# Splitting weight blocks ahead: a later split, a second raw place, one block per step

## The chip, the core and the metric

The kernel runs on one core of a Trainium2 chip. Its time is the device time of one execution in microseconds (us). The core has a matrix engine (PE, with its weight loads shown as PEld), three engines for elementwise work (DVE, ACT and POOL), and SP, whose queue issues nearly all DMAs of this kernel, one after the other. Each engine takes its instructions strictly in the order that the program gives it; semaphores make one wait for another.

## The reference, cut to what matters

Two groups of 2048 tokens pass through one encoder layer with shared weights:

```python
h = rms_norm(x, norm_w)
q_a, k_a, v_a, g_a, q_b, k_b, v_b, g_b = split(h @ w_in)     # 1024 x 3328
o_a = windowed_gqa_sink(rope(norm(q_a)), rope(norm(k_a)), v_a) * silu(g_a)
o_b = neighbourhood_attn(norm(q_b), norm(k_b), v_b, rpb_b) * silu(g_b)
x = x + concat([o_a, o_b]) @ w_out
y = x + (p @ w_ple) * sigmoid(x @ w_ple_gate)
```

Everything is float32. A product is formed from two parts of each operand: the rounded value (high) and what the rounding left (low), as three matmuls: high x high, high x low and low x high. So every operand, weights too, has to be split into two parts before PE can use it. A split of a 128x512 block is one ACT instruction (the high part) and one DVE instruction (raw minus high).

## The kernel before, in words

The work is a series of steps f, one for each block of 128 tokens. Steps 0 to 31 are stage A (projection and windowed attention of both groups). Steps 32 to 95 are stage B: 32 steps with the first half of the heads of group B, then 32 with the second half. A last stage, C, does the output projection and the gate.

The order of PE's instructions is fixed by a plan. A generator (`filler`) gives the projection matmuls of a step one by one, 24 to a projection. In stage B there are two projections per step: pqk (queries and keys, weights wa) and pvg (values and gates, weights wb). Between these matmuls the plan places the attention of a step six earlier: scores (scb), transposes of the probabilities (ptb), and the products with the values (pob). The attention hangs on DVE and ACT: DVE adds the bias to a score and takes the maximum (s, mx, line 263), ACT takes the exponential (s, line 279), ACT and DVE split the transposed probabilities (p_t, lines 838 and 839), and PE's pob needs p_t.

The rest of the engines' orders comes from a scheduler that keeps the program's priorities; a DMA is placed as early as its buffers allow.

The weight blocks that later stages need are split ahead, once, and their two parts are stored to DRAM (tensors named sp_...). This is `presplit` (lines 207 to 223). There are 44 such blocks: 28 of w_in for stage B, 4 of w_ple and 12 of w_out. `presplit(True)`, called at matmul 4 of a projection (PA), takes a tile "pre" of 128x3x512 with one buffer and loads a raw block of 256 KB into its third place. `presplit(False)`, 16 matmuls later in the same projection, has ACT and DVE write the two parts into the first two places, pinned behind the matmul that stands there (`behind`), and issues the store of 512 KB. As the tile has one buffer, the next load waits until that store has landed. In stage A one block is split per step, in steps 2 to 29.

From step 32 on a second user takes the same buffer (tag "raw"): `combine` (line 581) builds sums of the blocks of w_out and w_gate, eight of them, each in six moves: two loads of 512 KB, four POOL subtractions or additions, a store of 1 MB. One move is made per step, so it ends in step 80. Only then (`combined`) are the last 16 blocks split, in both projections of each step, two blocks per step, in steps 81 to 88.

Two steps at a change of weights run as a pair (`paired`): 62 and 63, between which the weights of the second half are loaded, and 94 and 95. In the latter pair the two 128x512 blocks of the first operand of p @ w_ple (p_r) are split as jobs between matmuls; `hold` counts how many matmuls pass before the first.

Other names: stx is a block of x on its way in; vb are values that are stored to DRAM (v_d) and loaded again as vw; o_tb is an output, stored to ob_d; kb and qg are normed keys and queries; q1b and q are the two parts of the queries.

Of the kernel before, what the change touches and what calls it, by code (L numbers as in the profile page):

```python
# [11 lines left out]
F32 = mybir.dt.float32  # L12
F32R = mybir.dt.float32r
# [6 lines left out]
NT = SEQ // 128  # L20
# [56 lines left out]
PA = 4  # L77
# [4 lines left out]
HOLD = {"wa": 20, "wb": 12, "wp": 0}  # L82
# [18 lines left out]
def emit(ctx, tc, io):  # L101
    nc = tc.nc
# [13 lines left out]
    nw = cp.tile([128, KT], F32, tag="nw", name="nw")  # L116
# [46 lines left out]
    jobs, hold, step = [], [0], [2]  # L163
# [16 lines left out]
    def w_block(half, tag, j):  # L180

        if half == "p":
            return io["w_ple"][128 * j:128 * j + 128, 512 * tag:512 * tag + 512]
        if half == "o":
            h, c = int(tag[2]) - 1, int(tag[1]) - 1
            return io["w_out"][512 * h + 128 * j:512 * h + 128 * j + 128, 512 * c:512 * c + 512]
        c0 = 1280 + 1024 * half + (512 if tag == "wb" else 0)
        return io["w_in"][128 * j:128 * j + 128, c0:c0 + 512]
# [13 lines left out]
            ws.append(w)  # L202
        return ws

    pre = []

    def presplit(load):

        if load:
            if to_split:  # L210
                pre.append((to_split.pop(0), ap.tile([128, 3, 512], F32R, tag="raw", name="pre", bufs=1)))
                nc.sync.dma_start(pre[-1][1][:, 2].bitcast(F32), w_block(*pre[-1][0]))
        elif pre:
            key, t = pre.pop()
            raw, sc = t[:, 2].bitcast(F32), nw[:, key[2]:key[2] + 1]
            if key[0] in ("p", "o"):
                behind(nc.scalar.copy(t[:, 0], raw))
                behind(nc.vector.tensor_tensor(out=t[:, 1], in0=raw, in1=t[:, 0].bitcast(F32), op=ALU.subtract))
            else:
                behind(nc.scalar.activation(t[:, 0], raw, AF.Copy, scale=sc))  # L220
                behind(nc.vector.scalar_tensor_tensor(out=t[:, 1], in0=raw, scalar=sc, in1=t[:, 0].bitcast(F32),
                                                      op0=ALU.mult, op1=ALU.subtract))
            nc.sync.dma_start(parts_d[key], t[:, 0:2].bitcast(F32))

    def load_first(st, j, c, n):

# [83 lines left out]
    ap = ab_stack.enter_context(tc.tile_pool(name="ab", bufs=1))  # L310
# [76 lines left out]
    raw = ap.tile([128, 4, 512], F32, tag="raw", name="ws", bufs=1)  # L387
# [23 lines left out]
    for i in range(2):  # L411
        square(1, i)
    blocks = [(half, tag, j) for half in range(2) for tag in ("wa", "wb") for j in range(KT)]
    parts_d = {(half, tag, j): dram.tile([128, 2, 512], F32, tag=f"sp_{half}{tag}{j}", name=f"sp_{half}{tag}{j}")
               for half, tag, j in blocks if half == 0 or tag == "wa" or j % 2 == 0}
# [3 lines left out]
    to_split = list(parts_d)  # L419
# [25 lines left out]
    for i in range(2):  # L445
        t = ap.tile([128, 2, 512], F32R, tag=f"q2{i}", name=f"q2{i}")
# [24 lines left out]
    def proj_a(f):  # L471
        s, t = divmod(f, NT)
# [80 lines left out]
        for i, c in enumerate(project(pg, xr, lambda k, b: w_g[k][:, b, :], 215)):  # L553
            if i in HG and f > 0 and not early:
                split(f + 1, HG[i], low=nc.vector if f == 1 else nc.gpsimd)
            if i in HN and f > 0 and f not in last:
                square(f + 1, HN[i])
            if i == PR:
                queries()
            if i in (PA, PA + 16) and 1 < f < 2 * NT - 2:  # L560
                presplit(i == PA)
            yield c
            if i + 24 == ka:
                keys_a(kt, t)
# [35 lines left out]
    combining, combined = combine(), []  # L600
# [106 lines left out]
    def proj_b(f):  # L707
        half, st = divmod(f - 2 * NT, 2 * NT)
        s, j = divmod(st, NT)
        b, cb = divmod(j, 4)  # L710
        if f < 2 * NT + 8:
            regroup_next()
        if not ks_b:
            ks_b.extend(big([128, 32, 2, 64], F32R, f"ks_b{e}") for e in range(2))
        w_qk, w_vg = w_b[half]
        xr = xt.pop(f)
        pk = ptile([128, 512], "pj", "pqk")
        for i, c in enumerate(project(pk, xr, lambda k, b: ready("wa", k, w_qk)[:, b, :], 215)):
            at = i + 24 if f in last else i
            if i == PD and f == 2 * NT + 9:  # L720
                stats_b(1)
            if at in HX:
                split(f + 1, HX[at])
            if i in (PA, PA + 16) and combined and f < 6 * NT - 2:
                presplit(i == PA)
            yield c
        sq = ap.tile([128, 512], F32, tag="sq", name="sqb", bufs=2)
        nc.scalar.activation(sq, pk, AF.Square)
        ssq = ap.tile([128, 8], F32, tag="ssq", name="ssqb", bufs=3)
        nc.vector.tensor_reduce(out=ssq, in_=sq.rearrange("p (h d) -> p h d", d=HD), op=ALU.add, axis=AX.X)  # L730
        vr = ap.tile([128, 8], F32, tag="vr", name="vrb", bufs=2)
        y = ap.tile([128, 8], F32, tag="y", name="yb", bufs=4)
        nc.vector.tensor_scalar(out=vr, in0=ssq, scalar1=1.0 / HD, scalar2=ep_b[:, st:st + 1],  # L733
                                op0=ALU.mult, op1=ALU.add)
        rsqrt(vr, y, 8)
        qg = ap.tile([128, 2, 4, HD], F32, tag="qg", name="qg", bufs=6)
        kt = ap.tile([128, 4, HD], F32, tag="kt", name="kb", bufs=2)
        def normed():

            for dst, c in ((kt, 4), (qg[:, 0], 0)):  # L740
                behind(nc.vector.tensor_tensor(out=dst, in0=pk[:, 64 * c:64 * c + 256].rearrange("p (h d) -> p h d", d=HD),
                                               in1=y[:, c:c + 4].unsqueeze(2).broadcast_to([128, 4, HD]), op=ALU.mult))
        yield 0, False
        pv = ptile([128, 512], "pj", "pvg")
        for i, c in enumerate(project(pv, xr, lambda k, b: ready("wb", k, w_vg)[:, b, :], 215)):
            if i + 24 in HX and f not in last:
                split(f + 1, HX[i + 24])
            if i == (PR if f not in last else 1):
                normed()
            if i in (PA, PA + 16) and combined and f < 6 * NT - 2:  # L750
                presplit(i == PA)
            yield c
            if i == (KB if f not in last else 10):
                if f < 2 * NT + 2:
                    pending.append((kt, b, cb))
                else:
                    keys_b(kt, b, cb)
        v = ap.tile([128, 4, 2, HD], F32R, tag="sq", name="vb", bufs=2)
        vp = pv[:, 0:256].rearrange("p (h d) -> p h d", d=HD)
        nc.scalar.activation(v[:, :, 0, :], vp, AF.Copy, scale=rs_b[:, st:st + 1])  # L760
        nc.vector.scalar_tensor_tensor(out=v[:, :, 1, :], in0=vp, scalar=rs_b[:, st:st + 1],
                                       in1=v[:, :, 0, :].bitcast(F32), op0=ALU.mult, op1=ALU.subtract)
        for w, (c0, ncol) in COL_WIN.items():
            lo, hi = max(c0, 16 * cb), min(c0 + ncol, 16 * cb + 16)
            if lo < hi:
                nc.sync.dma_start(v_d[half, s, w][8 * b:8 * b + 8, lo - c0:hi - c0].rearrange("r c h a d -> c r (h a d)"),
                                  v[8 * (lo - 16 * cb):8 * (hi - 16 * cb)].bitcast(F32).rearrange("p h a d -> p (h a d)"))
        gs = qg[:, 1].rearrange("p h d -> p (h d)")
        nc.scalar.activation(gs, pv[:, 256:512], AF.Tanh, scale=hr_b[:, st:st + 1])
        nc.vector.scalar_tensor_tensor(out=gs, in0=gs, scalar=1.0, in1=pv[:, 256:512], op0=ALU.add, op1=ALU.mult)  # L770
        held[f] = qg[:, 0], gs
        if next(combining, 0) == 0:
            combined.append(f)
        yield 0, False

    def prep_b(f):
# [195 lines left out]
    def paired(f, n):  # L972

        a, b = filler(f), filler(f + 1)
        half, w = (f - 2 * NT) // (2 * NT) + 1, []
        yield from islice(a, n)
        yield from islice(b, n)
        if half < 2:
            w.append(load_w(half, "wa"))
        else:  # L980
            load_early("p")
            hold[0], step[0] = HOLD["wa"], 2
        yield from a
        if half == 2:
            load_p(0)
            split_p(0, True)
            hold[0] = max(hold[0], HOLD["wb"])
        yield from b
        if half < 2:
            w.append(load_w(half, "wb"))  # L990
        else:
            for name in ("a11", "a12", "a22"):
                load_early(name)
        w_b[half] = w
# [43 lines left out]
    with tc.tile_pool(name="c", bufs=1, reuse_waits="tile") as op:  # L1038
# [190 lines left out]
        for m in range(7 * len(groups)):  # L1229
            n, i = divmod(m, 7)  # L1230
# [92 lines left out]
```

## Time and profile before

| what | value |
|---|---|
| median of 3 runs | 2507.85 us (2506.49 to 2507.91) |
| the profiled execution | 2506.79 us, span 2505.0 us, mean clock 0.999 |
| PE busy in the span | 2474.6 us (99%) |
| DVE, ACT, POOL busy | 1732.1, 1418.2, 782.1 us |
| moved by DMA | 438.86 MB, mean 175 GB/s |

The span is what the trace shows from the first instruction to the last; 1.8 us of the execution lie outside it, and the profiled execution is 1.06 us under the median. A step of stage B takes 15.5 to 17.3 us. A matmul's end is modelled in the trace, so PE reads as busy also where its matmuls only run into each other; stalls are seen better in how long the same instructions take in two places.

### The profile page before, as it was taken

What the parts mean: (1) busy time and instruction counts of PE and PEld (TensorE: products, weight loads), DVE (VectorE), ACT (ScalarE), POOL (GpSimd) and SP (SyncE); (2) the same over time, 40 slices, a digit from 0 to 9 for tenths busy, and PEclk for the clock granted to TensorE, in tenths of its full rate; (3) what the DMA queues carried; (4) which work ended last, traced back from release to release, by engine and by line L of the source; (5) the groups of instructions that cost most, each with busy time, mean ns of one, the idle gap of its engine ahead of it and who ended that gap; (6) DMA issues with size and microseconds to landing.
All of it is one profiled execution on the core that took longest, in us unless ns stands there. A gap on an engine that the chain in (4) does not pass through costs nothing.

```text
span 2505.0 us, 39845 instructions
## 1 busy us (share of the span) xinstructions
PE 2474.6 (99%) x12920; PEld 2087.5 (83%) x12920; DVE 1732.1 (69%) x4274; ACT 1418.2 (57%) x3341; POOL 782.1 (31%) x1033
## 2 busy tenths in 40 slices
PE   9999999999999999999999999999999999999999
PEld 7888888888888888888888887778788888888887
DVE  7777777777775666666666666666546655786776
ACT  6676767776764556666656556556664222354443
POOL 4444444444434444444444443333110000000000
PEclk9999999999999999999999999999999999999999
DMA  5433232222253565665955657666977455756765
GB/s 199 139 112 99 79 100 95 99 89 92 93 198 107 183 187 153 182 184 162 303 171 165 191 175 219 221 184 197 311 239 276 158 180 176 254 175 227 237 228 169
DMA packets 246657, 438.86 MB, mean 175 GB/s; under 512 B 31921, under 2 KB 86321, under 8 KB 241201
## 3 DMA queue, kind: packets, MB, share of 16 engines
q1 hardware_dynamic: 246160, 436.30, 54.0%
q8 instruction: 103, 1.69, 0.3%
q14 instruction: 106, 0.86, 0.1%
q10 hardware_dynamic: 288, 0.01, 0.0%
HBM read 308.28 MB, written 133.19 MB: 176 GB/s over the span
## 4 chain that ended last, share of the span: by engine, by line
PE 89%; DMA 4%; DVE 3%; ACT 2%; issue 1%; POOL 0%; SPq 0%; ACTq 0%; DVEq 0%; POOLq 0%
PE acca L1146 13%; PE pvg L248 12%; PE pqk L248 12%; PE accc L1146 10%; PE pg L248 7%; PE pq L248 7%; PE pk L248 4%; PE sc L248 3%; PE po L248 3%; PE scb L248 3%; PE pt L251 3%; PE ptb L251 3%; PE pob L248 3%; PE pple L248 3%; DMA pre<-w_out 1%
## 5 line engine op out<-in xcount | busy, mean ns | idle before, releaser
L279 ACT ACTIVATE s<-s,nm 128x384 f32<-128x384 f32 (+4 forms) x512 | 307.2, 601 | 324.1 <-DVE nm L274 194.9
L248 PE MATMUL pvg<-wb,xr 128*128 128x512 f32 x1536 | 462.7, 408 | 0.1
L248 PE MATMUL pqk<-wa,xr 128*128 128x512 f32 x1536 | 442.3, 410 | 0.0
L344 POOL TENSOR_TENSOR xr<-stx,xr 128x512 fp32r<-128x512 f32 x188 | 241.7, 1294 | 178.9 <-ACT xr L343 166.5
L248 PEld LDWEIGHTS pqk<-wa,xr 128*128 128x128 f32 x1536 | 266.3, 189 | 36.9
L248 PEld LDWEIGHTS pvg<-wb,xr 128*128 128x128 f32 x1536 | 267.7, 189 | 32.3 <-DVE wb L157 0.7
L1128 ACT CAST opd<-raw 128x512 fp32r<-128x512 f32 x224 | 131.5, 619 | 269.5 <-PE acca L1146 116.9
L1129 DVE TENSOR_TENSOR opd<-raw,opd 128x512 fp32r<-128x512 f32 x224 | 146.4, 685 | 145.2 <-ACT opd L1128 145.2
L248 PE MATMUL pg<-wb,xr 128*128 128x512 f32 x768 | 231.4, 409 | 1.0 <-DVE vv L494 1.0
L248 PE MATMUL pq<-wa,xr 128*128 128x512 f32 x768 | 220.3, 400 | 1.4 <-DVE wa L157 1.4
L263 DVE CUSTOM_DVE_ANT_0 s<-scb,bias 128x288 f32<-128x288 f32 (+3 forms) x256 | 140.9, 555 | 93.6 <-PE scb L248 88.8
L142 POOL TENSOR_TENSOR yb<-vrb,power 128x8 f32<-128x8 f32 x64 | 105.3, 1646 | 257.9 <-DVE vrb L733 257.9
L1146 PE MATMUL accc<-opd,wb 128*128 128x512 f32 x768 | 176.7, 389 | 0.0
L1146 PE MATMUL acca<-opd,wa 128*128 128x512 f32 x768 | 175.5, 389 | 0.0
L1146 PE MATMUL acca<-opd,s 128*128 128x512 f32 x768 | 175.4, 389 | 0.0
L1146 PEld LDWEIGHTS acca<-opd,wa 128*128 128x128 f32 x768 | 144.2, 188 | 29.9
L1146 PEld LDWEIGHTS accc<-opd,wb 128*128 128x128 f32 x768 | 144.2, 188 | 29.9
L1146 PEld LDWEIGHTS acca<-opd,s 128*128 128x128 f32 x768 | 144.2, 188 | 29.9
L858 DVE TENSOR_TENSOR otb<-pob,otb 64x512 f32<-64x512 f32 x128 | 88.2, 689 | 114.2 <-ACT otb L857 113.2
L248 PEld LDWEIGHTS pq<-wa,xr 128*128 128x128 f32 x768 | 139.1, 188 | 24.6 <-DVE wa L157 2.4
L248 PEld LDWEIGHTS pob<-p_t,vw 128*128 128x128 f32 (+2 forms) x832 | 132.4, 189 | 30.0 <-DVE p_t L839 8.7
L248 PEld LDWEIGHTS pg<-wb,xr 128*128 128x128 f32 x768 | 137.0, 189 | 21.9 <-DVE vv L494 1.5
(159 smaller groups left out, 5115.5 us busy)
## 6 DMA issues: line engine op xcount, KB each, us to landing
stx<-x_b SPq DMA_DIRECT2D x128, 256.0 KB
vw<-v_d SPq DMA_DIRECT2D x112, 256.0 KB
stx<-x_a SPq DMA_DIRECT2D x64, 256.0 KB
stn<-x_n SPq DMA_DIRECT2D x64, 256.0 KB
v_d<-vb SPq DMA_DIRECT2D x64, 256.0 KB
ple_d<-ev SPq DMA_DIRECT2D x64, 256.0 KB
xres<-x_r SPq DMA_DIRECT2D x64, 256.0 KB
x_d<-r SPq DMA_DIRECT2D x64, 256.0 KB
```

What stands on the lines that cost most here:

```text
L142: nc.gpsimd.tensor_tensor(out=y, in0=v, in1=power.broadcast_to([128, n]), op=ALU.pow)
L248: pinned(nc.tensor.matmul(out, lhsT, rhs, start=start, stop=stop))
L251: pinned(nc.tensor.transpose(out, in_, eye))
L263: nc.vector.tensor_tensor_reduce(out=s[:, :n], in0=ps[:, :n], in1=bias, scale=1.0, scalar=-3.0e38, op0=ALU.add, op1=ALU.max, accum_out=sm[ ...
L279: ex = nc.scalar.activation(ss[i][:, :n], ss[i][:, :n], AF.Exp, bias=nm[:, i:i + 1], accum_out=den[:, i:i + 1])
L344: low.tensor_tensor(out=lo, in0=raw, in1=hi.bitcast(F32), op=ALU.subtract)
L858: nc.vector.tensor_tensor(out=ot[a:a + 64], in0=pq[a:a + 64], in1=ot[a:a + 64], op=ALU.add)
L1128: P(nc.scalar.copy(hi, v))
L1129: P(nc.vector.tensor_tensor(out=lo, in0=v, in1=hi.bitcast(F32), op=ALU.subtract))
L1146: pinned(nc.tensor.matmul(ps, w[k][:, a, c:c + 128], o[:, b], start=i in (0, 1, 4) and k == 0 and j == 0, stop=k == 3 and j == 2, skip_gro ...
```

## The change

The change has four parts.

1. One tile "pre" of 128x4x512 is kept over many blocks in place of a new tile for each. Raw blocks go into its third and fourth place in turn. The store of a block is no longer issued behind its split, but at the next call of `presplit(True)`, ahead of the next load. A function `store_last` issues the last store of stage A, in step 30, and gives the tile up.
2. In stage B `presplit(True)` is called at matmul 4 of pqk and `presplit(False)` at matmul 20 of pvg, 40 matmuls later. One block is split per step.
3. `combine` makes two moves in every step with f % 8 == 4 instead of one. It ends in step 75, and the 16 blocks are split in steps 76 to 91; the last store is due in step 92.
4. In the last pair, `hold` is set to 16 where it was 12 at that point.

```diff
-    pre = []
+    pre, due = [], []
     def presplit(load):
         if load:
+            if due:
+                key, t, slot = due.pop()
+                nc.sync.dma_start(parts_d[key], t[:, 0:2].bitcast(F32))
             if to_split:
-                pre.append((to_split.pop(0), ap.tile([128, 3, 512], F32R, tag="raw", name="pre", bufs=1)))
-                nc.sync.dma_start(pre[-1][1][:, 2].bitcast(F32), w_block(*pre[-1][0]))
-        elif pre:
-            key, t = pre.pop()
-            raw, sc = t[:, 2].bitcast(F32), nw[:, key[2]:key[2] + 1]
+                if not pre:
+                    pre.extend([ap.tile([128, 4, 512], F32R, tag="raw", name="pre", bufs=1), 0])
+                pre[1] += 1
+                due.append((to_split.pop(0), pre[0], 2 + pre[1] % 2))
+                key, t, slot = due[0]
+                nc.sync.dma_start(t[:, slot].bitcast(F32), w_block(*key))
+        elif due:
+            key, t, slot = due[0]
+            raw, sc = t[:, slot].bitcast(F32), nw[:, key[2]:key[2] + 1]
...
-            nc.sync.dma_start(parts_d[key], t[:, 0:2].bitcast(F32))
+
+    def store_last():
+        key, t, slot = due.pop()
+        nc.sync.dma_start(parts_d[key], t[:, 0:2].bitcast(F32))
+        pre.clear()
...
+            if i == PA and f == 2 * NT - 2:
+                store_last()
...
-            if i in (PA, PA + 16) and combined and f < 6 * NT - 2:
-                presplit(i == PA)
+            if i == PA and combined and (to_split or due):
+                presplit(True)
...
-            if i in (PA, PA + 16) and combined and f < 6 * NT - 2:
-                presplit(i == PA)
+            if i == PA + 16:
+                presplit(False)
...
-        if next(combining, 0) == 0:
-            combined.append(f)
+        for _ in range(2 if f % 8 == 4 else 1):
+            if next(combining, 0) == 0:
+                combined.append(f)
...
-            hold[0] = max(hold[0], HOLD["wb"])
+            hold[0] = 16
```

PE's instructions stand in the same order in both kernels. Three places of the other engines follow. First SP in stage B, among the blocks of w_out, before: between an output (ob_d) and the loads of values (vw) two blocks pass, each a store (sp_oa) and the load of the next.

```order
L867 DMA ob_d_90<-o_tb 128x2x128
L223 DMA sp_oa_234<-pre 128x1024
L766 DMA v_d_301<-vb 8x8x512
L766 DMA v_d_302<-vb 16x8x512
L212 DMA pre<-w_out 128x512
L326 DMA stx<-x_b 128x512 x2
L223 DMA sp_oa_235<-pre 128x1024
L212 DMA pre<-w_out 128x512
L810 DMA vw<-v_d_298 96x512
```

The same queue in the changed kernel, from one output to the next but one store:

```order
L882 DMA ob_d_90<-o_tb 128x2x128
L212 DMA sp_oa_233<-pre 128x1024
L219 DMA pre<-w_out 128x512
L780 DMA v_d_299<-vb 16x8x512
L780 DMA v_d_300<-vb 8x8x512
L338 DMA stx<-x_b 128x512 x2
L825 DMA vw<-v_d_298 120x512 x2
L825 DMA vw<-v_d_295 96x512 x2
L821 DMA bias<-bias 128x4x384
L882 DMA ob_d_90<-o_tb 128x2x128
L212 DMA sp_oa_234<-pre 128x1024
```

One block passes per step; the load that stands behind a store fills the other raw place, for the split after the next. It no longer waits for that store.

Second, SP where the weights wb of the second half of stage B are loaded (steps 63 and 64), before. The raw blocks of `combine` are loaded ahead of wb; wb's second and later blocks stand behind the stores of values (v_d), which wait for DVE.

```order
L589 DMA raw<-w_gate 128x1024 x2
L810 DMA vw<-v_d_292 128x512 x2
L326 DMA stx<-x_b 128x512 x2
L867 DMA ob_d_91<-o_tb 128x2x128
L197 DMA wb_15651<-sp_1wb_225 128x1024
L766 DMA v_d_293<-vb 8x8x512
L766 DMA v_d_294<-vb 16x8x512
L200 DMA wb_15653<-pl_1wb_245 128x512
L197 DMA wb_15655<-sp_1wb_226 128x1024
L200 DMA wb_15657<-pl_1wb_246 128x512
```

And now:

```order
L882 DMA ob_d_91<-o_tb 128x2x128
L197 DMA wb_15628<-sp_1wb_225 128x1024
L200 DMA wb_15630<-pl_1wb_245 128x512
L197 DMA wb_15632<-sp_1wb_226 128x1024
L780 DMA v_d_293<-vb 8x8x512
L780 DMA v_d_294<-vb 16x8x512
L610 DMA sums_250<-raw 128x2048
L200 DMA wb_15634<-pl_1wb_246 128x512
L197 DMA wb_15636<-sp_1wb_227 128x1024
```

Three blocks of wb moved ahead of the v_d stores; the 1 MB store of `combine` moved in front of the fourth, and its loads left this place.

Third, DVE at the end of step 77, before (q and qg are queries, p_t the split probabilities that pob waits for):

```order
L289 RECIPROCAL rd<-den 128x4
L290 TENSOR_SCALAR rd<-rd,hr_b 128x4
L786 SCALAR_TENSOR_TENSOR q_281<-pqtb,wk,q1b 64x256
L741 TENSOR_TENSOR qg<-pqk,yb 128x256
L786 SCALAR_TENSOR_TENSOR q_281<-pqtb,wk,q1b 64x256
L839 TENSOR_TENSOR p_t<-ptb,p_t 120x288
```

And now:

```order
L301 RECIPROCAL rd<-den 128x4
L302 TENSOR_SCALAR rd<-rd,hr_b 128x4
L801 SCALAR_TENSOR_TENSOR q_281<-pqtb,wk,q1b 64x256
L755 TENSOR_TENSOR qg<-pqk,yb 128x256
L225 TENSOR_TENSOR pre<-pre 128x512
L801 SCALAR_TENSOR_TENSOR q_281<-pqtb,wk,q1b 64x256
L854 TENSOR_TENSOR p_t<-ptb,p_t 120x288
```

The split's DVE half stands between the two query parts, ahead of the first p_t. It stands so in nearly all of the 16 steps, and it stood so in step 81 before. The fourth part of the change moves no instruction on any engine: the rows of p_r stand among the same neighbours in both kernels.

## The prediction

> **What bounds the kernel now.** I read the page first, then the chain of waits, then stretches of stage B against each other, then the waits inside the slow stretch.
>
> ```profile
> span 2505.0 us, 39845 instructions
> PE 2474.6 (99%) x12920; PEld 2087.5 (83%) x12920; DVE 1732.1 (69%) x4274; ACT 1418.2 (57%) x3341; POOL 782.1 (31%) x1033
> PE 89%; DMA 4%; DVE 3%; ACT 2%; issue 1%; POOL 0%; SPq 0%; ACTq 0%; DVEq 0%; POOLq 0%
> ```
>
> PE bounds the kernel: its order is fixed and the change leaves it alone, so time can only come from places where PE stands still. The chain of what ended last has 4% of the span in DMAs. Read in order of time it shows a run of them in stage B (start, length, what):
>
> ```profile
> 1522.65 0.83 DVE pre L218
> 1523.49 4.18 DMA sp_p<-pre
> 1527.74 3.56 DMA pre<-w_ple
> 1531.32 0.63 ACT pre L217
> ```
>
> This is the one-buffered tile going round: a split's DVE half, the store that must land (4.18 us), only then the load (3.56 us), then the next split. One round takes 9.3 us, and stage B wants two in a step of 16.5 us, whose split points are fixed in PE's order. ACT is in-order, so when the split's place comes before the data, everything behind it on ACT waits, and DVE with it. What that costs PE is seen by setting steps 82 to 89 beside steps 66 to 73, whose shapes are the same (the pattern repeats every 16 steps). Columns: the stretch, its length, busy time of each engine with its instructions, clock, DMA share, GB/s.
>
> ```profile
> 1263.87:1389.70 125.83, 125.83 (x692) 106.05 (x690) 84.58 (x226) 76.72 (x186) 58.77 (x63) 1.00 0.55 170
> 1521.82:1663.87 142.05, 130.84 (x692) 106.62 (x690) 93.15 (x241) 84.70 (x200) 51.34 (x57) 0.99 0.68 218
> ```
>
> Both hold the same 692 matmuls. The second takes 142.05 - 125.83 = 16.2 us longer. The waits inside it say why (who waited for whom: total, times, longest):
>
> ```profile
> PE scb L248 <- DVE mx L263: 5.8, 4, 2.3
> PE pob L248 <- DVE p_t L839: 3.7, 5, 1.2
> PE ptb L251 <- ACT s L279: 1.1, 2, 0.9
> PE pgtb L251 <- DVE mx L263: 0.6, 1, 0.6
> ACT pre L217 <- DMA pre<-w_out: 19.4, 8, 4.4
> ACT pre L217 <- DMA pre<-w_ple: 3.2, 1, 3.2
> DVE pre L218 <- ACT pre L217: 20.2, 9, 4.3
> ```
>
> PE stands for 11.2 us, always for DVE or ACT work, and these stand 20.2 and 22.6 us for the split's data. In steps 66 to 73 PE has no wait at all that the trace lists. The rest of the 16.2 us is matmuls that refill after each stop, and a stretch at a lower clock (below).
>
> **The change part by part.** *Stage B, load and store taken out of the way: -16.2 us.* A load now fills the other raw place and needs only the split two blocks earlier; by the order of SP it stands right behind the store before, some one and a half steps (about 24 us) ahead of its own split. Against that stand 3.56 us of load. A split still has to wait for the store of the block before it, since both write the same two places; that store is issued behind the previous split, a step ahead (about 15 us), and took 4.18 us. Both are covered more than three times. Two blocks in 16.5 us become one. So no split should find its data missing, and the whole excess goes. SP has two DMAs less per step in steps 81 to 88 and two more in 76 to 80 and 89 to 91; it waits as now behind DVE at the store. The bytes are the same.
>
> *The splits themselves: +1.7 us.* All 16 now stand at matmul 20 of pvg, between the two query parts on DVE. A split without missing data stood there once before, in step 81:
>
> ```profile
> 1520.71 0.60 ACT L217 CAST pre<-pre 128x512 fp32r<-128x512 f32 x1
> 1522.65 0.82 DVE L218 TENSOR_TENSOR pre<-pre 128x512 fp32r<-128x512 f32 x1
> 1523.50 0.49 DVE L786 SCALAR_TENSOR_TENSOR q<-pqtb,wk,q1b 64x256 fp32r<-64x256 f32 x1
> 1524.02 0.46 DVE L839 TENSOR_TENSOR p_t<-ptb,p_t 120x288 fp32r<-120x288 f32 x1
> 1523.64 0.95 PE L248 MATMUL pqk<-wa,xr 128*128 128x512 f32 x3
> 1524.94 1.12 PE L248 MATMUL pqk<-wa,xr 128*128 128x512 f32 x4
> ```
>
> and the same place of step 66, without a split:
>
> ```profile
> 1265.33 0.46 DVE L839 TENSOR_TENSOR p_t<-ptb,p_t 120x288 fp32r<-120x288 f32 x1
> 1265.69 0.95 PE L248 MATMUL pqk<-wa,xr 128*128 128x512 f32 x3
> 1266.78 1.13 PE L248 MATMUL pqk<-wa,xr 128*128 128x512 f32 x4
> ```
>
> From the step's start (1521.82 and 1263.87) p_t comes 2.20 us in, against 1.46: 0.74 us late. PE's two groups of pqk, with pob between them, stand 1.30 apart against 1.09: PE loses 0.21 us, the other 0.53 us of the delay are slack. The bounds for 16 splits are 0 and 16 x 0.74 = 11.8 us (no slack anywhere). The measured place gives 16 x 0.21 = 3.4. In six of the 16 steps the split stands one place earlier on DVE, where it fills an idle spell, and the slack of a step's first p_t varies with its shape, so I take half, 1.7 us.
>
> *Stage A: 0.* One block per step, as before. In a typical step there the store and the load of "pre" are issued like this, and the split follows:
>
> ```profile
> 266.05 0.33 SPq L223 DMA_DIRECT2D sp_0wb<-pre  x1
> 269.93 0.38 SPq L212 DMA_DIRECT2D pre<-w_in  x1
> 287.49 0.73 ACT L220 ACTIVATE pre<-pre,nw 128x512 fp32r<-128x512 f32 x1
> ```
>
> The load has 17.6 us before ACT uses it, and ACT did not idle ahead of that (its row has no wait). The new order only lets it come earlier; the store is as early as it was. The cover is the projection of a whole step; were it gone, it would cost what it costs stage B. SP's loads of stn stand at most three places later.
>
> *`combine`, two moves in every eighth step: 0.* Two of the six double steps put two POOL operations on one step. Their price is one POOL operation, taken from the like-sized subtraction in this row (mean 1294 ns), so 2.6 us at most:
>
> ```profile
> L344 POOL TENSOR_TENSOR xr<-stx,xr 128x512 fp32r<-128x512 f32 x188 | 241.7, 1294 | 178.9 <-ACT xr L343 166.5
> L142 POOL TENSOR_TENSOR yb<-vrb,power 128x8 f32<-128x8 f32 x64 | 105.3, 1646 | 257.9 <-DVE vrb L733 257.9
> ```
>
> POOL idles 257.9 us ahead of 64 of its yb, 4.0 us each, which covers 1.3.
>
> *The change of weights at step 64: 0, between -1.9 and +2.7.* Here `combine`'s transfers move against the loads of wb. Rows of SP, the chain, PE, and step 64 against step 80:
>
> ```profile
> 1231.74 1.17 SPq L766 DMA_DIRECT2D v_d<-vb  x2
> 1232.96 0.58 SPq L200 DMA_DIRECT2D wb<-pl_1wb  x1
> 1234.13 5.64 DMA wb<-pl_1wb
> 1228.25:1247.35 19.10, 18.21 (x98) 14.08 (x96) 13.72 (x31) 12.55 (x27) 7.96 (x8) 1.00 0.94 321
> 1488.05:1505.29 17.24, 17.24 (x97) 14.43 (x96) 11.52 (x29) 10.08 (x23) 6.47 (x8) 1.00 0.62 199
> 1240.00:1244.00 4.00, 4.00 (x23) 3.09 (x22) 3.42 (x11) 2.21 (x4) 1.65 (x1) 1.00 1.00 382
> ```
>
> Step 64 is 1.86 us longer than step 80 for late wb. Two more blocks of wb now go ahead of the wait at 1231.74, and 1 MB of raw loads is gone from in front of them: at best all 1.86 us go. But a 1 MB store stands in front of the fourth block: 1.05 MB at the 382 GB/s of the last row is 2.7 us. Ahead of that block stood 1.05 MB before (v_d and two of wb), and 1.3 MB now (v_d and the sums), so the two roughly cancel, and I take 0.
>
> *`hold`: 0.* No instruction stands elsewhere for it, so nothing can move.
>
> **Sum**, against the profiled execution: 2506.79 - 16.2 + 1.7 = 2492.3; against the median, which is 1.06 us higher, 2493.4.
>
> **The clock.** Part of the 16.2 us is a lower clock of PE (the number ahead of the last two):
>
> ```profile
> 1584.00:1588.00 4.00, 1.68 (x11) 1.33 (x10) 1.61 (x5) 1.22 (x2) 0.00 (x0) 1.00 0.11 39
> 1588.00:1592.00 4.00, 4.00 (x15) 3.23 (x14) 2.60 (x11) 2.40 (x8) 2.06 (x2) 0.58 0.54 180
> 1776.00:1780.00 4.00, 1.77 (x9) 1.10 (x7) 1.34 (x2) 2.25 (x4) 0.00 (x0) 1.00 1.05 395
> ```
>
> It follows a stop of 2.3 us; the loss is (1 - 0.58) x 4.00 = 1.7 us. I count it with the stops. The third row shows a longer stop that did not lower it. [...]
>
> **The rivals.** (a) *The lower clock is not the stops' and stays.* For it: the stop of 1776 to 1780 lowered nothing. Against: it is the only such stretch between the start and the end, and stands right behind the longest stop of the slow steps. 2493.4 + 1.7 = 2495.1. (b) *The 1 MB store delays wb at step 64.* For it: a DMA share of 0.94 there. Against: two blocks of wb go earlier. 2493.4 + 2.7 = 2496.1. (c) *The splits cost their full delay*, DVE becoming the bound of each step's start: 2507.85 - 16.2 + 11.8 = 2503.5, no change by the measure below. Against: slack of 0.53 us in the one clean place. (d) *The stops remain*, because the split now waits for its store where it waited for its load: then nothing moves, 2507.9. Against: a step between them. (e) *Slower: vw loads come late.* A store now stands on SP in each of 16 steps, waiting for DVE's split, with the stores of v_d and up to four vw loads behind it that pob needs. SP waits there now (total, times, longest):
>
> ```profile
> SPq L223 <- DVE pre L218: 26.8, 11, 5.2
> ```
>
> Yet none of PE's waits quoted above names a DMA, with vw behind such waits. It decides at 14.5 / 16 = 0.9 us of lost time per step; at 1.5 us per step the time is 2507.85 - 14.5 + 24 = 2517.
>
> **How the numbers follow.** Chances: forecast 0.65 (2489 to 2498 for itself), (a) 0.08, (b) 0.10, (c) 0.07, (d) 0.05, (e) 0.05. The range runs from 2489 (all of step 64's excess gone as well: 2507.85 - 16.2 - 1.9 = 2489.8, less what the lowest run lies under the median) to 2499.5 (splits at 3.4 and the store's 2.7 on top: 2507.85 - 16.2 + 3.4 + 2.7 = 2497.8, and (a) on top of that); it holds the forecast, (a) and (b), 0.83. No change means within 0.2%, 5.0 us, which is about what a measurement of this kernel can tell. Faster: forecast, (a), (b): 0.83. Same: (c), (d): 0.12. Slower: (e): 0.05.
>
> **What would show it.** Right: ACT's waits for loads of "pre" gone, steps 82 to 89 at 126 to 128 us, no lower clock near 1588, step 64 at 17 to 20 us, stage A's steps unchanged. Wrong: ACT waiting for sp_ stores at the split, PE's pob waiting for vw, or pob late by more than 0.2 us in many steps from 77 on.

## The result and the profile after

The changed kernel takes 2496.53 us (median of 4 runs, 2493.45 to 2497.78) against 2507.88 us (4 runs of the kernel before). The ratio is 0.9953, with a 95% interval of 0.9935 to 0.997. Beside other kernels on another occasion it took 2495.75 us (5 runs), ratio 0.995 (0.9937 to 0.9964). So it is faster by half a per cent, 11 to 12 us. The forecast was 2493.4, with a range of 2489 to 2499.5.

The profiled execution is the fastest of the four. From its page, the span, the engines and the chain of waits:

```profile
span 2491.5 us, 39866 instructions
PE 2470.3 (99%) x12920; PEld 2084.8 (84%) x12920; DVE 1733.7 (70%) x4274; ACT 1417.0 (57%) x3341; POOL 786.7 (32%) x1033
PE 93%; DMA 3%; DVE 2%; ACT 1%; issue 1%; POOL 0%; SPq 0%; DVEq 0%; ACTq 0%; POOLq 0%
```

PE carries 93% of the chain in place of 89%. Where the time went is read from stretches that hold the same work. The changed kernel: steps 82 to 89, steps 76 to 93, steps 64 to 75, and step 64 alone.

```profile
1524.57:1650.66 126.09, 126.09 (x691) 105.99 (x690) 88.86 (x234) 80.52 (x194) 53.34 (x57) 1.00 0.64 202
1424.05:1716.97 292.92, 292.89 (x1599) 245.30 (x1597) 204.04 (x521) 183.60 (x430) 119.81 (x128) 1.00 0.62 193
1230.33:1424.05 193.72, 192.93 (x1051) 161.26 (x1050) 131.04 (x341) 118.78 (x281) 87.09 (x93) 1.00 0.63 198
1230.33:1249.45 19.12, 18.33 (x98) 14.11 (x96) 13.57 (x31) 12.35 (x27) 6.71 (x7) 1.00 0.96 332
```

The kernel before: steps 76 to 93 and steps 64 to 75 (its steps 82 to 89 took 142.05 us and its step 64 took 19.10).

```profile
1421.98:1729.90 307.92, 296.70 (x1598) 246.23 (x1597) 203.78 (x521) 185.21 (x430) 120.29 (x132) 0.99 0.62 189
1228.25:1421.98 193.73, 192.84 (x1051) 161.25 (x1050) 131.01 (x341) 118.85 (x281) 87.08 (x93) 1.00 0.62 194
```

Steps 76 to 93, where the blocks are split, are 307.92 - 292.92 = 15.0 us shorter. Steps 82 to 89 come to 126.09 us, against 125.83 in steps 66 to 73 that hold no split. In that stretch of the changed kernel no wait for "pre" is left in the list of waits. The only one of PE for an engine is this (total, times, longest):

```profile
PEld pob L260 <- DVE p_t L854: 0.8, 3, 0.4
```

The weights change and `combine`'s double moves cost nothing (193.72 against 193.73).

But the changed kernel reaches stage B 2.0 us late, at 724.20 in place of 722.20. Nearly all of it, 1.9 us, arises in steps 15 and 16. These steps before:

```profile
333.74:356.85 23.11, 23.11 (x134) 20.26 (x133) 18.13 (x55) 16.26 (x44) 10.29 (x17) 1.00 0.37 92
356.85:379.96 23.11, 23.11 (x134) 20.26 (x133) 18.14 (x55) 16.26 (x44) 10.30 (x17) 1.00 0.27 92
```

And after:

```profile
333.75:357.39 23.64, 23.30 (x134) 20.23 (x133) 17.55 (x51) 14.09 (x35) 8.92 (x14) 1.00 0.48 90
357.39:381.90 24.51, 23.36 (x134) 20.30 (x133) 18.58 (x58) 17.98 (x53) 11.67 (x21) 1.00 0.27 87
```

SP's rows there show what moved. Before (start, length, line, what):

```profile
338.85 0.33 SPq L326 DMA_DIRECT2D stn<-x_n  x1
339.28 0.38 SPq L212 DMA_DIRECT2D pre<-w_in  x1
340.10 0.33 SPq L326 DMA_DIRECT2D stn<-x_n  x1
340.52 0.38 SPq L604 DMA_DIRECT2D ms_d<-ms_a  x1
```

After:

```profile
336.28 0.80 SPq L219 DMA_DIRECT2D pre<-w_in  x1
338.86 0.33 SPq L338 DMA_DIRECT2D stn<-x_n  x1
339.29 0.39 SPq L618 DMA_DIRECT2D ms_d<-ms_a  x1
340.12 1.51 SPq L338 DMA_DIRECT2D stn<-x_n  x1
```

`regroup` stores ms_d (2048 means of squares, each an element of 4 bytes) once for each of the two groups of tokens. Before, both loads of stn went ahead of that store. Now the load of "pre" goes early, since its place is free, and ms_d comes between the two stn loads. A piece of the chain of waits (start, length), and then the waits of the changed kernel in these two steps:

```profile
340.12 13.79 DMA stn<-x_n
```

```profile
ACT stn L369 <- DMA stn<-x_n: 4.0, 1, 4.0
PE pt L263 <- DVE ot L702: 1.1, 1, 1.1
```

The second stn load takes 13.79 us. ACT stands 4.0 us for it, and what is queued behind on ACT (keys, exponentials) is late for DVE and then for PE.

The remaining 0.6 us of the gain lie behind step 93. They are mostly a stop of PE at the start of the embeddings. The wait before, and after:

```profile
PE ptb L251 <- ACT s L279: 3.3, 1, 3.3
```

```profile
PE ptb L263 <- ACT s L291: 2.9, 1, 2.9
```

That stop matters below. The sum of the profiled executions: -15.0 + 2.0 - 0.6 = -13.6; the spans differ by 13.5.

### The profile page after: what moved, and what is told of

It is laid out like the page before. It is cut to its first block, busy times and chain, and to the rows that moved or that the text cites. A ratio compares the mean times of both kernels' runs of the same rounds, so it can differ in the third digit from the quotient of the medians.

```text
span 2491.5 us, 39866 instructions
## 1 busy us (share of the span) xinstructions
PE 2470.3 (99%) x12920; PEld 2084.8 (84%) x12920; DVE 1733.7 (70%) x4274; ACT 1417.0 (57%) x3341; POOL 786.7 (32%) x1033
## 4 chain that ended last, share of the span: by engine, by line
PE 93%; DMA 3%; DVE 2%; ACT 1%; issue 1%; POOL 0%; SPq 0%; DVEq 0%; ACTq 0%; POOLq 0%
PE pvg L260 14%; PE pqk L260 14%; PE acca L1161 13%; PE accc L1161 10%; PE pg L260 7%; PE pq L260 7%; PE scb L260 3%; PE ptb L263 3%; PE sc L260 3%; PE po L260 3%; PE pob L260 3%; PE pk L260 3%; PE pt L263 3%; PE pple L260 3%; DMA p<-p_t 1%; DMA stn<-x_n 1%
```

## The experiments

In the expectations "steps 14 and 15" are counted from the trace's first separable step; they are the steps 15 and 16 of this text. "The stop at the start of the embeddings" is a place near 1766 us (1779 in the kernel before) where PE waits for an exponential that is queued on ACT behind p_r, the split of the next tile's p. In the first profile of the changed kernel ACT's row of p_r there, with the wait ahead of it, is:

```profile
1764.23 1.38 ACT L905 CAST p_r<-p 128x512 fp32r<-128x512 f32 x2 [1.25 <-DMA p<-p_t]
```

**The changed kernel once more.** No edit.

> The changed kernel once more, beside the three below on the same chip. Theory S (its later runs, 2 to 4 us above the first, had a mean clock of 0.999 and stopped somewhere that the profiled execution did not): runs between 2493 and 2498, and if this profile falls among the slow ones, one or two stretches of about 4 us at half clock, each behind a stop of 2 to 4 us, 1.7 us each. Rival N (plain scatter of the transfers): no half-clock stretch in a profile of 2496 or more; many steps a few hundredths of a microsecond longer.

2495.75 us (2494.93 to 2497.51); the profiled execution was 2497.51. Against the first profile it is 1.3 us later at the end of the first step and 2.9 us longer between the embeddings' first matmul and stage C's (129.44 against 126.54). The loss in steps 15 and 16 is there again (23.63 and 24.47 us). The stop at the embeddings, from the waits, and slices of 4 us around it:

```profile
PE ptb L263 <- ACT s L291: 3.6, 1, 3.6
```

```profile
1764.00:1768.00 4.00, 2.26 (x12) 1.52 (x10) 1.03 (x2) 1.85 (x5) 0.00 (x0) 1.00 1.05 396
1768.00:1772.00 4.00, 2.15 (x7) 1.80 (x8) 1.84 (x5) 3.95 (x11) 0.92 (x2) 0.56 0.77 288
1772.00:1776.00 4.00, 4.00 (x18) 3.48 (x17) 2.19 (x5) 2.55 (x7) 1.22 (x3) 0.59 0.45 165
```

The first profile has a clock of 1.00 in the same place, behind a stop of 2.9 us. So theory S holds for this execution: a longer stop and two slices near half clock. It is one profile of a longer execution. A low clock at this place does not by itself make an execution a long one: the kernels with a second raw place alone and with one block a step, below, show it (0.57 in one slice of 4 us, and 0.82 and 0.75 in two) in profiles that are faster than their own medians (2493.33 against 2493.88 us, and 2493.78 against 2494.18).

**A second raw place alone.**

```diff
 # the kernel before, with
-                pre.append((to_split.pop(0), ap.tile([128, 3, 512], F32R, tag="raw", name="pre", bufs=1)))
+                if not place:
+                    place.extend([ap.tile([128, 4, 512], F32R, tag="raw", name="pre", bufs=1), 0])
+                place[1] += 1
+                pre.append((to_split.pop(0), place[0], 2 + place[1] % 2))
```

> The kernel before with nothing changed but a second raw place in one lasting tile: a load fills the place that the last split did not read; splits stay two a step in steps 81 to 88, 16 matmuls behind their load, each store right behind its split. Theory R (the 16.2 us are the round store 4.2 us, load 3.6 us, split 1.5 us of the one buffer, against 8.3 us that a half step offers): load and store now overlap, the longer of them is 4.2 us, so the stops go: steps 82 to 89 at 126 to 129 us, time 2491 to 2495. Rival D (what counts is the 40 matmuls between load and split): the load is still issued behind the store before it, so the split still finds its data missing in most half steps: steps 82 to 89 above 135 us, time above 2500.

2493.88 us (2492.32 to 2495.01), ratio 0.9942 (0.9929 to 0.9954). Steps 82 to 89 and 76 to 93:

```profile
1523.19:1649.24 126.05, 126.05 (x691) 106.01 (x690) 93.05 (x241) 83.70 (x200) 53.32 (x57) 1.00 0.76 243
1423.37:1715.30 291.93, 291.93 (x1599) 245.66 (x1597) 203.78 (x521) 184.41 (x430) 122.29 (x132) 1.00 0.65 200
```

Theory R. With two blocks a step and 16 matmuls between load and split, a second raw place in a lasting tile makes the stops go as well. The later split and the slower pace are not needed for it. Steps 76 to 93 are even 1.0 us shorter than in the changed kernel. In stage A half of the loss remains (step 16 takes 24.05 us): here, too, the load of "pre" finds a free place early.

**The changed kernel with one raw place.**

```diff
-                due.append((to_split.pop(0), pre[0], 2 + pre[1] % 2))
+                due.append((to_split.pop(0), pre[0], 2))
```

> The changed kernel with one raw place instead of two (the lasting tile, 40 matmuls, one block a step, the store issued with the next load all stay). Theory R with the split's end as the release: the place is free as soon as the split before has read it, 32 matmuls (11 us) ahead of the load, so nothing waits: as the changed kernel, within 1 us. Rival P (the second place is what does it): the load waits again for something of the block before, stops come back: 5 to 16 us slower than the changed kernel.

2495.87 us (2493.86 to 2497.59), 0.1 us from the changed kernel on the same occasion. Steps 82 to 89:

```profile
1524.57:1650.66 126.09, 126.09 (x692) 106.02 (x690) 88.83 (x234) 80.56 (x194) 53.36 (x57) 1.00 0.64 202
```

126.09 us again: at one block a step and with the lasting tile, the second place is not needed. A load then waits only for the split that read the raw place, not for the store of the two parts: the one issued at 1541.55 has 13.8 us until ACT's half of its split at 1555.33. Whether a lasting tile with one raw place is enough at two blocks a step was not run.

**One block a step alone.**

```diff
 # the kernel before, with
-            if i in (PA, PA + 16) and combined and f < 6 * NT - 2:     (in the projection pqk)
-                presplit(i == PA)
...
-        if next(combining, 0) == 0:
-            combined.append(f)
+        for _ in range(2 if f % 8 == 4 else 1):
+            if next(combining, 0) == 0:
+                combined.append(f)
```

> The kernel before with one block a step in stage B: the splits at pqk are left out, combine goes two moves in every eighth step so that the 16 blocks run from step 76 to 91; the one buffer, the 16 matmuls between load and split and the store right behind the split stay, and stage A is that of the kernel before. Theory R (the loss is two rounds of 9.3 us in a step of 16.5): one round has room, so no stop is left: steps 76 to 93 as in the changed kernel within 1 us, stage B starting at 722; 2490 to 2496. Rival D (distance or a second place is needed): ACT waits for loads of pre in most steps from 76 on, some 1 us of PE per step, 2500 or more.

2494.18 us (2493.46 to 2496.59), ratio 0.9947 (0.9933 to 0.996). Steps 76 to 93:

```profile
1422.34:1715.26 292.92, 292.89 (x1598) 245.30 (x1597) 204.09 (x521) 183.57 (x430) 119.76 (x128) 1.00 0.62 194
```

292.92 us, to the hundredth the changed kernel's time, with the one buffer, the short distance and the store right behind the split. So the pace alone does it too. The cause of the 16.2 us is what a second raw place and the slower pace both remove: two rounds of store, load and split through one buffer in one step. Either way out is enough. The longer distance between load and split, and a lasting tile with one raw place, were not run by themselves at two blocks a step.

**Stage A as before.**

```diff
 # the changed kernel, with the old presplit for stage A
-                presplit(i == PA)
-            if i == PA and f == 2 * NT - 2:
-                store_last()
+                presplit_a(i == PA)
```

> The changed kernel in stage B, the kernel before in stage A (a tile for each block, load and split 16 matmuls apart, store right behind the split). Theory Q (the 1.9 us lost in steps 14 and 15 come from the order on SP: the second stn load stands behind the store of ms_d, 2048 elements of 4 bytes, since the load of pre goes first): the loss goes, step 15 back to 23.1 us, first matmul of stage B at 722.2 us instead of 724.2, time 1.5 to 2.5 us below the changed kernel on the same chip, near 2492 in a run at full clock. Rival V (the two steps scatter by that much in any run): stage B starts at 724 as before, or the changed kernel's second profile starts at 722 by itself.

2494.83 us (2493.16 to 2497.52), which is within the scatter of the changed kernel's 2495.75. The trace is plainer than the times. Steps 15 and 16:

```profile
335.57:358.69 23.12, 23.12 (x135) 20.26 (x133) 18.15 (x55) 16.29 (x44) 10.29 (x17) 1.00 0.38 92
358.69:381.80 23.11, 23.11 (x134) 20.26 (x133) 18.14 (x55) 16.27 (x44) 10.28 (x17) 1.00 0.26 92
```

The loss is gone, as theory Q has it. Stage B starts at 724.07 all the same, since this execution had lost 1.9 us by the end of its first step. The 2.5 us forecast at most for the time did not show: a low clock (0.57 over 4 us at the embeddings, 1.7 us) and the start (1.9 us) scatter by as much as the effect.

**The store of ms_d from another queue.**

```diff
-        nc.sync.dma_start(ms_d[s * SEQ:(s + 1) * SEQ].rearrange("(t p) -> p t", p=128), ms_a[:, c])
+        nc.scalar.dma_start(ms_d[s * SEQ:(s + 1) * SEQ].rearrange("(t p) -> p t", p=128), ms_a[:, c])
```

> The changed kernel with the two stores of ms_d (2048 elements of 4 bytes each) issued from ACT's queue instead of SP's; SP's order is otherwise the same. Theory Q1 (a load on the same queue waits behind the elements of that store): the second stn load of step 15 lands in about 3 us instead of 13.8, steps 14 and 15 back to 23.11 us each, 1.9 us less than the changed kernel. Rival Q2 (the elements fill the 16 DMA engines whatever the queue): the stn load still takes 8 us or more and the steps stay at 23.6 and 24.5.

2493.66 us (2492.01 to 2495.73), ratio 0.9943 (0.993 to 0.9956). Steps 15 and 16, then SP's and ACT's rows there:

```profile
333.76:356.88 23.12, 23.12 (x135) 20.26 (x133) 17.72 (x52) 15.81 (x42) 10.29 (x17) 1.00 0.61 92
356.88:379.99 23.11, 23.11 (x134) 20.26 (x133) 18.53 (x58) 16.47 (x46) 10.30 (x17) 1.00 0.28 92
```

```profile
338.88 1.58 SPq L338 DMA_DIRECT2D stn<-x_n  x2
```

```profile
338.92 0.41 ACTq L618 DMA_DIRECT2D ms_d<-ms_a  x1
351.76 0.63 ACT L369 ACTIVATE stn<-stn 128x512 f32<-128x512 f32 x1 [1.81 <-DMA stn<-x_n]
```

Both steps are back at 23.11, and stage B starts at 722.19. But the load is not fast. SP's two issues end at 340.46, and ACT gets the second block at 351.76, 11.3 us later; in the changed kernel it got it at 353.99. So neither theory is right in full. The elements slow the load from another queue also (Q2), by most of what they do on the same one: from the end of SP's issue it takes 11.3 us here and 12.4 in the changed kernel (from 340.12 + 1.51 = 341.63 to 353.99); a load of the same 256 KB, one of "pre", took 3.56 us in the kernel before. The 2.2 us won are what counts, as they bring ACT's wait from 4.0 to 1.8 us, which the slack behind it covers. SP's issues end at 340.46 in place of 341.63, so 1.2 of the 2.2 us are issue time; where the other 1.0 comes from is open.

**The splits left out.** 15 of the 16 splits of stage B are not computed here; loads and stores stay.

```diff
-        elif due:
+        elif due and len(to_split) >= 15:
```

> The changed kernel without 15 of the 16 splits of stage B: ACT's and DVE's half of the splits in steps 77 to 91 are left out, loads and stores stay (the blocks stored are not the split weights). Theory W (the splits cost PE 0 to 0.3 us each, as the steps 76 to 92 of the two traces suggest): steps 77 to 92 together 0.8 to 1.6 us shorter than in the changed kernel. Rival F (the splits are free; what is longer is due to the stores and loads): within 0.2 us. By the prediction's term, 1.7 us.

2497.99 us (2496.2 to 2499.31), no faster than with the splits. Steps 79 to 92 are shorter, as expected. The changed kernel, then this one:

```profile
1473.91:1700.44 226.53, 226.50 (x1232) 189.41 (x1231) 159.04 (x406) 142.43 (x335) 93.18 (x98) 1.00 0.62 196
```

```profile
1477.68:1703.33 225.65, 225.65 (x1233) 189.77 (x1231) 151.10 (x392) 136.50 (x322) 88.97 (x98) 1.00 0.56 172
```

226.53 - 225.65 = 0.88 us for 13 splits: theory W. The cost is not spread evenly. Steps 80, 81, 82 and 92 are longer with the splits by 0.24, 0.16, 0.17 and 0.26 us, the other ten by 0.06 at most.

Steps 77 and 78 lost 4.0 us, though. SP's rows ahead of them, the longest wait of SP and the wait of PE there:

```profile
1431.34 9.57 SPq L219 DMA_DIRECT2D pre<-w_out  x4
1441.01 1.82 SPq L825 DMA_DIRECT2D vw<-v_d  x4
```

```profile
SPq L219 <- DMA pre<-w_out: 10.8, 4, 3.4
PE pob L260 <- DMA vw<-v_d: 2.4, 3, 1.4
```

With no split to read a block, nothing held its load back. The loads were placed early and in a bunch, each waiting on SP for the one that filled its place last. Four vw loads stood behind them, issued at 1441.01 where the changed kernel has 1436.44, and PE waited 2.4 us for them. So vw came late behind waits on SP, as in the slower rival (e), though here the waits are those of loads for each other and not of a store for DVE's split.

**a22 loaded later.**

```diff
-            for name in ("a11", "a12", "a22"):
+            for name in ("a11", "a12"):
                 load_early(name)
...
+            if m == 2 and n == 1:          (in the embeddings' loop)
+                load_early("a22")
```

> The changed kernel with the four loads of a22 (2 MB) taken from the run of loads at the end of stage B and issued in the second embeddings tile. Theory S (the stop of 2.9 to 3.6 us at the start of the embeddings is ACT waiting for the next tile's p, queued behind 2 MB and more of such loads; a stop above some 3.4 us halves the clock for about 4 us behind it): the stop falls below 2 us, no half clock near 1770, time 2 to 4 us under the changed kernel, and its runs closer together. Rival T (the stop is the embeddings' stores and vw, not a22): the stop stays at 2.9 or more; or the loads of a22 in the second tile make a stop there of the same size, and the time stays.

2494.03 us (2490.75 to 2498.88): too wide to tell from the changed kernel. The stop moved, as the trace shows. The longest wait of PE at the start is now 1.7 us, without a low clock behind it; but a short stop for vw at 1785 (1.3 us, and 0.35 right behind it) has one.

```profile
PE pob L260 <- DMA vw<-v_d: 1.9, 3, 1.3
PE scb L260 <- DVE mx L275: 1.7, 1, 1.7
```

```profile
1784.00:1788.00 4.00, 2.38 (x13) 1.60 (x12) 1.69 (x4) 2.10 (x5) 1.09 (x3) 1.00 1.08 320
1788.00:1792.00 4.00, 4.00 (x15) 3.34 (x14) 1.14 (x2) 1.83 (x4) 0.00 (x0) 0.57 0.97 352
```

S is right that these loads feed the stop: they stand right ahead of p on SP, and without them p is issued at 1754.02 instead of 1756.66 us and split from 1759.51 instead of 1764.23, ahead of the exponentials. ACT's own wait for p is no shorter for it (3.1 us instead of 1.25); it has only moved to where nothing hangs on it. S is wrong that some 3.4 us of stop are needed for the lower clock: the stops at the embeddings fitted it in the six profiles taken until then (2.9, 3.3 and 3.3 us left the clock at 1.00, 3.4, 3.5 and 3.6 lowered it), but here 0.57 follows 1.3 us, and 0.58 followed 2.3 us near 1588 in the kernel before.

**The best of it.** The second place alone with ms_d from ACT's queue; and the same with a11, a12 and a22 spread over three embeddings tiles.

```diff
 # both: the kernel with a second raw place alone, with
-        nc.sync.dma_start(ms_d[s * SEQ:(s + 1) * SEQ]...
+        nc.scalar.dma_start(ms_d[s * SEQ:(s + 1) * SEQ]...
 # one of them also
-            for name in ("a11", "a12", "a22"):
-                load_early(name)
...
+            if m == 2 and 0 < n < 4:
+                load_early(("a11", "a12", "a22")[n - 1])
```

> The kernel before with a second raw place (splits two a step in steps 81 to 88, as before) and with the stores of ms_d from ACT's queue. Theory Q1 with R: stage A as in the kernel before (stage B starts at 722, less what the start of the run scatters), no stop in stage B, and the splits cost 0.2 us in all where they stand two a step, against 1.2 us spread over 16 steps: the embeddings start 15.3 to 15.8 us earlier than in the kernel before, 1746.4 to 1747; time about 2507.9 - 15.5 = 2492.4. Rival: the 0.9 us between the two spreadings was the scatter of one trace: the embeddings start no earlier than 1747.3 with the same start of the run.

> As the kernel of the other run of this pair (second raw place alone, ms_d from ACT's queue), and a11, a12 and a22 (2 MB each) are loaded in the second, third and fourth embeddings tile instead of at the end of stage B. Theory S2 (the stops at the start of the embeddings, 5 us of PE in 40 us and now and then a half clock on top, are p and vw queued behind 6 MB of these loads): PE busy above 39 of 40 us behind the first embeddings matmul, no half clock there, first matmul of stage C 120 to 124 us behind the first of the embeddings (126.5 to 129.4 so far), time 3 to 6 us under the other run: 2486 to 2490. Rival T2 (the loads collide with something wherever they stand): new stops for vw, p or the blocks themselves later in the embeddings, and less than 1 us gained.

Without the spread loads: 2492.21 us (2491.18 to 2492.97), ratio 0.9933 (0.992 to 0.9945). Steps 76 to 93:

```profile
1421.23:1713.17 291.94, 291.94 (x1598) 245.68 (x1597) 203.76 (x521) 184.38 (x430) 122.28 (x132) 1.00 0.64 200
```

291.94 us, as in the first kernel with splits in pairs (291.93) and the one with the loads spread (291.98). The seven profiles with one block a step and all splits have 292.92 to 292.99, so the difference of 1.0 us is the place of the splits, not scatter. It lies in steps 77, 78, 80, 81 and 92, which are 0.12, 0.17, 0.24, 0.16 and 0.27 us shorter here than in the changed kernel: with the splits in steps 81 to 88, none stands at the end of the step before one of these. The embeddings start at 1745.45, 16.7 us earlier than in the kernel before and 1 us earlier than expected. Half of that is a step 64 of 18.58 us; the kernel with the loads spread, which is the same up to there, takes 19.27, so that half is scatter.

With the spread loads: 2489.47 us (2487.88 to 2491.72), ratio 0.9924 (0.991 to 0.9937), some 7 us faster than the changed kernel and the fastest here. The 40 us behind the first embeddings matmul, without and with the spread:

```profile
1745.45:1785.45 40.00, 35.04 (x187) 28.82 (x186) 21.24 (x51) 25.22 (x57) 5.30 (x10) 0.96 0.88 293
```

```profile
1746.58:1786.58 40.00, 37.09 (x206) 30.58 (x205) 23.22 (x55) 27.76 (x63) 5.31 (x10) 1.00 0.98 340
```

PE is busy 37.1 of 40 us instead of 35.0, the clock is whole, and stage C starts 124.9 us behind the embeddings instead of 128.1. Of these 3.2 us, 1.7 are a low clock that the execution without the spread happened to have (0.59 and 0.98 in two slices of 4 us). Both theories are partly right. The wait for the exponential is gone with those loads, and the time lies in S2's 2486 to 2490; but PE was not busy above 39 us, stage C was not reached within 124, and the gain is 2.7 us and not 3 to 6. What remains is mainly one wait of 1.9 us for vw.

## Why the prediction was right, and where not

*Stage B, the stops: -16.2.* Right, in mechanism and size: no wait for "pre" is left and steps 82 to 89 are within 0.3 us of steps without splits. The reasoning by which it was said to go (a load one and a half steps ahead, a second place, one block a step) took all three to be at work; the runs show that the second place in a lasting tile is enough alone, and so is one block a step. The longer lead was not run alone.

*The splits: +1.7, in bounds of 0 to 11.8.* Measured: 16.2 - 15.0 = 1.2, of which leaving the splits out shows 0.88 in 13 of the steps. Half of the clean place's 0.21 for each split was near the sum, and its reason, slack that varies with the step, fits: a few steps pay about the clean place's price, most pay nothing. That this came to about a half was luck. What the prediction did not ask is what the old places cost: in pairs, in steps 81 to 88 and free of missing data, the splits cost 1.0 us less. So the third part of the change, slowing the pace to one block a step, costs 1.0 us once the buffer is mended.

*Stage A: 0.* This step failed: it measured +2.0. The prediction saw the move ("SP's loads of stn stand at most three places later") and priced it at nothing, as if each place were a DMA like the others. One of the places was behind ms_d, whose 2048 elements of 4 bytes hold up what follows: the load issued behind it took 13.79 us, while the same load ahead of it, in the kernel before, was issued at 340.10 and used without a wait at 349.82, so within 9.7 us. The loss occurs only at the end of the first group of tokens, and a typical step, from which the prediction argued, does not have it. Two edits that leave the rest alone took the loss away.

*combine, the change of weights: 0 and 0.* Right: 193.72 against 193.73 us, and step 64 at 19.12 against 19.10. That the two sides of the 1 MB store cancel was a guess that came out; neither side was tested by itself, and the agreement to 0.02 us is luck, as step 64 took 18.58 and 19.27 us in two kernels that are the same up to there. *hold: 0.* Nothing speaks against it; it was not run alone.

*The sum.* For the profiled execution 2492.3 was forecast and 2493.45 measured: +2.0 in stage A, -0.5 at the splits, -0.6 behind step 93, with 0.3 unresolved. That the errors have opposite signs is luck. The median lies 3.1 us above that profile and not 1.1 as assumed. In the one longer execution that was looked at (2497.51 us), the start of the run (1.3 us) and the embeddings (2.9 us, with a clock of 0.56 and 0.59 in two slices of 4 us) explain the excess.

*The clock.* The stretch near 1588 went with its stop (the first profile of the changed kernel reads 1.00 in every slice of 8 us up to 2484), so counting it with the stops was right, and rival (a) is out for this stretch. It was not foreseen that the stop at the embeddings, with 1.00 behind it in the profile of before, has a lower clock behind it in other executions (0.56 and 0.59 in the changed kernel's second profile).

*Rivals.* (b), a late wb: step 64 is unchanged. (c) and (d): steps 82 to 89 rule both out. (e), vw behind stores: not in this kernel; the kernel without splits shows that vw late on SP costs PE time, 4.0 us in two steps.

## What to carry to other kernels

When a buffer's round is longer than the time between its uses, count the round first: here a second raw place and a slower pace each ended it, and only one need be paid for. When a load moves on a queue, look at every step for what then changes places behind it, and above all at the rare transfers (a store of single elements, a burst of weights), since a typical step does not show them. An effect of 2 us is read from the length of the same steps in two traces; runs that scatter by 4 us hide it.

## What the runs showed of the hardware

Of the fourteen stops listed here, those below 3.4 us leave the clock whole in some cases and have a low clock behind them in others. The fourteen are the stop of PE at the start of the embeddings or its longest one near it in each of the twelve profiles, the short one of "a22 loaded later", and the one near 1588 of the kernel before:

| the clock behind the stop | stops, us (kernel) |
|---|---|
| stays at 1.00 | 1.7 (a22 later), 1.9 (loads spread), 2.9 (changed), 3.3 (before), 3.3 (one raw place) |
| falls, once | 1.3 (a22 later), 2.3 (before, near 1588), 2.7 (second place, ms_d from ACT), 2.9 (one block a step), 3.4 (stage A as before), 3.5 (second place alone) |
| falls, for twice as long | 3.4 (changed, ms_d from ACT), 3.6 (changed, second profile), 3.8 (splits left out) |

All five stops of 3.4 us or more are followed by a low clock, and four of the nine shorter ones. The row of "one block a step" and the slices there are these:

```profile
PE ptb L251 <- ACT s L279: 2.9, 1, 2.9
```

```profile
1764.00:1768.00 4.00, 2.00 (x9) 1.61 (x10) 1.68 (x5) 3.95 (x10) 0.77 (x2) 0.82 1.01 376
1768.00:1772.00 4.00, 4.00 (x21) 3.34 (x20) 2.50 (x5) 2.91 (x7) 1.38 (x3) 0.75 0.50 179
```

What is alike is how deep the clock falls and how long it stays low. In slices of 0.5 us the stretch near 1588 of the kernel before reads 0.98, six times 0.50, and 0.61 (from 1587.5 on), which makes (0.02 + 6 x 0.50 + 0.39) x 0.5 / 0.5 = 3.4 us at 0.50. The four others read in such slices (the changed kernel's second profile, "stage A as before", "one block a step", "a22 later") are at 0.50 between their ends as well. By the same measure in slices of 4 us, 0.57 is 0.43 x 4 / 0.5 = 3.4 us; 0.82 and 0.75 make (0.18 + 0.25) x 4 / 0.5 = 3.4; 0.56 and 0.59 make 6.8, twice that. The others come to 3.4 or 6.8 as well. What besides its length decides whether a low clock follows a stop was not shown: one follows the 1.3 + 0.35 us of "a22 later", and none follows either stop of 3.3 us.
